# A hybrid decoder step on one core: accumulators from another PSUM pool, gate samples by pairs of heads, three output groups by ScalarE and TensorE

## The chip, the core and the metric

The kernel runs on one core of one Trainium2 chip. A core has five engines that run their own instruction queues: TensorE (PE: matrix products; its weight loads are listed apart as PEld), VectorE (DVE), ScalarE (ACT), GpSimd (POOL) and SyncE (SP, which here issues DMAs). TensorE writes its products into PSUM, eight banks of 128 partitions x 512 f32. The metric is device time in microseconds (us), from several runs; a profile is one further execution, with every instruction's start and duration.

## The reference

One layer of a decoder, D = 2048, on 256 new prompt tokens and 8 sequences of 8 new tokens each, the samples. The kernel treats the 320 tokens together.

```python
h = rms_norm(x, norm_mix_pre)
a_u, a_v, z, xbc, dt_raw = split(h @ w_in)                    # 2048 -> 9248 columns
gate_out = gelu(a_u) * (tril(W_s) @ layer_norm(gelu(a_v)) + b_s)   # 16 heads of 128, chunks of 128 tokens
ssm_out  = rms_norm_by_group(ssd_scan(silu(conv(xbc)), dt, state) * silu(z))   # 4 groups
x = x + rms_norm([gate_out | ssm_out] @ w_out, norm_mix_post)
f = (gelu(g) * u) @ w_down,   [g | u] = conv(rms_norm(x) @ w_up)    # D_FF = 5632
y = x + rms_norm(f, norm_ffn_post)
```

In the gate a sample has 8 tokens, so its mixing matrix is the upper left 8 x 8 of W_s; all samples of a head are one product with a block-diagonal 64 x 64 matrix. The outputs are y, the new states and the last rows of the convolutions and of the gate's v.

## The kernel before, in words

**Products.** Activations lie transposed (features on partitions, 320 tokens along the free dimension). Each f32 product is made of three passes on rounded parts (`accumulate`, L131): whi x xhi (L134), whi x xlo (L135), wlo x xhi (L136). Weights come in slabs of 128 x 1024 (`slab`, L109): SP loads the raw slab, ScalarE rounds it to whi (L123), VectorE takes the difference wlo (L124). A slab serves 24 passes; there are three buffers of each.

**PSUM.** Two pools of four banks each: `mm` (tag "mm", L53) and `ms` (tag "ms", L54; `misc`, L56, takes a bank of it). `mm` holds the four accumulators of a projection (`project`, L175) or, one after the other, the sixteen of an output chunk. `ms` serves the smaller products: the gate's (`sg`), those of the state scan (`xt_ps`, `s1_ps`, `yo_ps`, `cb_ps`, `up_ps`, `y_ps`), sums and spreads.

**Output chunks.** `chunk_out` (L234) multiplies four 128-row blocks of one part of the mix (or of the FFN's inner vector) with 512 rows of w_out (or w_down): for each of sixteen output blocks nb it takes an accumulator from `mm`, runs 12 passes, and VectorE adds it to `acc` (L247). Chunks 0 to 2 are the gate's first three quarters, chunk 3 its last, chunks 4 to 7 the four groups of the scan.

**Order of the work around the change.** After the gate the main line is: the convolution's input projection of group 1 (`heads_in`, through `conv_proj`, L439), chunk 3, z of group 0 (`heads_out`), projection of group 2, chunk 4, z of group 1, projection of group 3, chunk 5, z of groups 2 and 3, chunk 6, chunk 7. At the end of a `conv_proj` its four `mm` banks are taken over by `evac`: VectorE multiplies them into `pad` (L452 the prompt, L453 the samples, after which the bank is free), then ScalarE and VectorE run the convolution (L457, L459). The scan of each group (`ssd`, L888) is a background task, advanced a step at a time by `tick` between slabs; it takes `ms` banks for `ps_x`, `s1_ps` and `yo_ps` (read last by L915 and L1011) and for `up_ps` and `y_ps`. The final order on each engine is made by a planner from dependencies, priorities (`first()` is the highest) and a cost model, with the explicit `issue_after` edges.

**Gate.** `layer_norm` (L749) normalises v, tokens on partitions: `vt` has three row blocks, two of 128 prompt tokens and one of the 64 samples, of which the upper 64 partitions are zeroed once by GpSimd (L729). It goes by quarters of 512 columns (q) and row blocks (c) with two VectorE instructions each (L772, L773). `gate_mix(g, ...)` (L785) handles four heads: it loads their mixing matrices, masks them (L795 for the prompt's wT, L797 for the samples' wS, whose upper half is zero), and per head runs two prompt products (L806), one sample product of 64 columns (L807), all into one `ms` bank, and VectorE adds the bias and multiplies by u. Two heads go per step of the background task; the last group of four heads runs in one go ahead of chunk 3's projection. An f32 product that is not split into parts shows as two instructions of TensorE.

**Last norm.** In the last chunk every finished block of f is scaled by its weight and turned by VectorE into token order (`f_tok`, ten groups of 32 tokens, 128 x 512 each; `x1_tok` likewise). After the sum of squares (L1391, L1394), VectorE and ScalarE make the root r for each group (L1396 to L281). Then y = f r + x: seven groups by VectorE in one instruction each (L1417), groups 2, 5 and 8 by ScalarE (f r, L1410) and GpSimd (+ x, L1412). Each finished group is sent by a DMA (L1423), VectorE's from SP's queue and the others from ScalarE's.

Of the kernel before, what the change touches and what calls it, by code (L numbers as in the profile page):

```python
# [8 lines left out]
F32 = mybir.dt.float32  # L9
# [3 lines left out]
ALU = mybir.AluOpType  # L13
# [3 lines left out]
P = 128  # L17
NP = 256
NB, TS = 8, 8
# [14 lines left out]
def hybrid_step(  # L34
# [21 lines left out]
    def misc(name):  # L56
        return ms.tile([P, 512], F32, tag="ms", name=name)
# [173 lines left out]

        return (slice(0, P), slice(P, NT)) if nb == KD - 1 else (slice(0, NT),)

    def chunk_out(w, ck, hi, lo, begins, done=None, rate=1, apart=False):  # L234

        for nb in range(KD):
            if nb % 2 == 0:
                wb = slab(rows_of(w, 4 * ck, 4, P * nb, 256))
            ps = mm.tile([P, 512], F32, tag="mm", name=f"pd_{ck}_{nb}")
            for k in range(4):  # L240
                made = accumulate(ps[:, :NT], wb(k, nb % 2), hi[:, k, :], lo[:, k, :], k == 0, k == 3)
            with first():
                if begins:
                    act.copy(acc[:, nb, :], ps[:, :NT])
                else:
                    for ts in parts_of(nb) if apart else (slice(0, NT),):
                        added_last[:] = [dve.tensor_tensor(out=acc[:, nb, ts], in0=acc[:, nb, ts], in1=ps[:, ts], op=ALU.add).ins]  # L247
# [184 lines left out]
    with ExitStack() as mctx:  # L432
# [158 lines left out]
        with tc.tile_pool(name="gp", bufs=1) as gp:  # L591
# [157 lines left out]
            def layer_norm():  # L749

                mv = gp.tile([P, 3, 2], F32, name="mv")
                pool.memset(mv, 1.0)
                while v_task in side:
                    yield 24, 0
                for c, (o, n) in enumerate(TOK):
                    dve.bn_aggr(mv[:n, c, :], bn[c][:n].rearrange("p a b -> p (a b)"))
                lr = rsqrt_of(mv[:, :, 1], 1.0, 3)
                rows = []

                def load(q):  # L760
                    cs = slice(512 * q, 512 * q + 512)
                    for name, src in (("lg", gate_ln_g), ("lb", gate_ln_b)):
                        rows.append(gp.tile([P, 512], F32, tag=name, name=name, bufs=2))
                        with tc.issue_after(behind_r1[0]):
                            pool.dma_start(rows[-1], src[0:1, cs].broadcast_to([P, 512]))
                load(0)
                load(1)
                yield
                for q in range(4):
                    for c, (o, n) in enumerate(TOK):  # L770
                        v = vt[:n, c, 512 * q:512 * q + 512]
                        dve.scalar_tensor_tensor(out=v, in0=v, scalar=mv[:n, c, 0:1], in1=rows[2 * q][:n], op0=ALU.subtract, op1=ALU.mult)  # L772
                        dve.scalar_tensor_tensor(out=v, in0=v, scalar=lr[:n, c:c + 1], in1=rows[2 * q + 1][:n], op0=ALU.mult, op1=ALU.add)  # L773
# [10 lines left out]

            def gate_mix(g, uf, res):  # L785
                wT = gp.tile([P, 4, P], F32, tag="wT", name="wT", bufs=1)
                w8 = gp.tile([NS, 4, TS], F32, tag="w8", name="w8", bufs=1)
# [12 lines left out]
                hi, lo = out_parts(hp, "o")  # L800
                res += hi, lo
                for j in range(4):
                    fs = slice(512 * g + P * j, 512 * g + P * j + P)
                    ps = misc("sg")
                    for c in range(2):
                        pe.matmul(ps[:, P * c:P * c + P], vt[:, c, fs], wT[:, j, :], start=True, stop=True)  # L806
                    pe.matmul(ps[:, NP:NT], vt[:, 2, fs], wS[:, j].rearrange("p b t -> p (b t)"), start=True, stop=True)  # L807
                    s = tp.tile([P, NT], F32, tag="ev", name="s", bufs=2)
                    dve.tensor_tensor(out=s[:, :NP].rearrange("p (c t) -> p c t", c=2),
                                      in0=ps[:, :NP].rearrange("p (c t) -> p c t", c=2),  # L810
                                      in1=bs[:, j, :].unsqueeze(1).to_broadcast([P, 2, P]), op=ALU.add)
                    dve.tensor_tensor(out=s[:, NP:].rearrange("p (b t) -> p b t", b=NB),
                                      in0=ps[:, NP:NT].rearrange("p (b t) -> p b t", b=NB),
                                      in1=bs[:, j, :TS].unsqueeze(1).to_broadcast([P, NB, TS]), op=ALU.add)
                    dve.tensor_tensor(out=s, in0=s, in1=uf[:, j, :], op=ALU.mult)
                    split(hi[:, j, :], lo[:, j, :], s)
                    if j % 2:
                        yield

            normed = layer_norm()  # L820
            bg.append(normed)
# [32 lines left out]
        with tc.tile_pool(name="sd", bufs=1) as sd:  # L854
# [331 lines left out]
            chunk_out(w_out, 4, *res[0], False)  # L1186
            norm = heads_out(1)
            heads_in_next(3)
            finish(norm)
            chunk_out(w_out, 5, *res[1], False)  # L1190
            norm = heads_out(2)
            norm3 = heads_out(3)
            finish(norm)
            chunk_out(w_out, 6, *res[2], False)
            finish(norm3)
            finish(tasks[3])
            sq2 = hp.tile([P, NT], F32, tag="ssq", name="sq2")
# [74 lines left out]
    with tc.tile_pool(name="fp", bufs=1) as fp:  # L1272
# [129 lines left out]
        @contextmanager  # L1402
        def behind(eng):

            with tc.issue_after(taken[eng]) if eng in taken else nullcontext():
                yield

        for c in BY_POOL:
            with behind("act"):
                taken["act"] = act.activation(f[:, c], f[:, c], AF.Copy, scale=r[:, c:c + 1]).ins  # L1410
            with behind("pool"):
                taken["pool"] = pool.tensor_tensor(out=f[:, c], in0=f[:, c], in1=x[:, c], op=ALU.add).ins  # L1412
        for c in range(SN):
            if c in BY_POOL:
                continue
            with behind("dve"):
                taken["dve"] = dve.scalar_tensor_tensor(out=f[:, c], in0=f[:, c], scalar=r[:, c:c + 1], in1=x[:, c],  # L1417
                                                        op0=ALU.mult, op1=ALU.add).ins
        for eng, queue in (("sp", sp), ("act", act)):
            for c in range(SN):  # L1420
                if (c in BY_POOL) == (eng == "act"):
                    with behind(eng):
                        taken[eng] = queue.dma_start(o_y[:, c], f[:, c]).ins  # L1423


_OUTS = [
# [8 lines left out]
def laid_out(a):  # L1435
# [7 lines left out]
    def states(v, n):  # L1443
# [19 lines left out]
        "gate_w8": np.concatenate([w8] * NB),  # L1463
# [43 lines left out]
```

## Time and profile before

| | |
|---|---|
| time, median of 3 runs | 1756.57 us (1756.36 to 1757.76) |
| the profiled execution: its time / its span, first to last instruction | 1756.8 / 1755.1 us |
| granted TensorE clock, mean | 0.997 |
| HBM read / written | 280.51 / 19.69 MB |
| mean rate of the DMA queues | 172 GB/s |

The profile counts time from the first instruction. A line such as `L453 DVE TENSOR_TENSOR pad<-ps,r` is the instruction made by line 453, on VectorE, writing the tile `pad` from `ps` and `r`. "x24" is a count; what stands in square brackets is the idle time of the engine before it and the instruction whose end released it. A listed duration of a TensorE product contains its way through the array, so products overlap; the distance from one start to the next is the time that it takes from the engine.

### The profile page before, as it was taken

The numbers are of one execution on the slowest core, as the hardware profiler recorded it, in microseconds if no ns is written. First come the engines' busy times: TensorE is split into PE (matmuls) and PEld (weight loads), VectorE is DVE, ScalarE is ACT, GpSimd is POOL, SyncE is SP. The second block draws the span as 40 slices with busy tenths as digits, with TensorE's granted clock in tenths as the row PEclk, the third lists the DMA queues.
The fourth block names the chain that finished last, engine by engine and source line by source line (L and its number), as shares of the span: only waits on it lengthen the run. The fifth ranks groups of instructions, "written<-read, shape, count | busy, mean of one in ns | idle before, by whom it ended". The sixth has DMA issues, their size and how long they took to land.

```text
span 1755.1 us, 31141 instructions
## 1 busy us (share of the span) xinstructions
PE 1738.4 (99%) x12079; PEld 1720.6 (98%) x12079; DVE 1181.1 (67%) x2015; ACT 820.0 (47%) x1199; POOL 328.5 (19%) x686
## 2 busy tenths in 40 slices
PE   9999999999999999999999999999999999999996
PEld 9999999999999999999999999999999999999996
DVE  6559864656969787778855566565657565656487
ACT  6344544334656565645544434343434343343435
POOL 2532330000423323112210101010202010101003
PEclk9999999999999999999999999999999999999998
DMA  7786565456566676665654545545454545454543
GB/s 241 240 235 177 180 177 155 154 161 194 190 210 202 214 220 190 213 197 162 187 157 146 156 148 154 150 148 156 151 153 148 156 149 150 153 154 148 152 152 108
DMA packets 227171, 302.24 MB, mean 172 GB/s; under 512 B 21328, under 2 KB 151504, under 8 KB 226832
## 3 DMA queue, kind: packets, MB, share of 16 engines
q1 hardware_dynamic: 210976, 272.42, 51.1%
q0 software_dynamic: 6176, 13.84, 2.6%
q10 hardware_dynamic: 9872, 14.00, 2.2%
q8 instruction: 95, 1.56, 0.4%
q14 instruction: 52, 0.43, 0.1%
HBM read 280.51 MB, written 19.69 MB: 171 GB/s over the span
## 4 chain that ended last, share of the span: by engine, by line
PE 60%; DVE 1%; issue 0%; DVEq 0%; ACT 0%
PE ps L134 13%; PE ps L135 12%; PE ps L136 12%; PE pd L134 7%; PE pd L136 7%; PE pd L135 7%; DVE f_tok L1417 0%; PE fin_ps L1134 0%; PE y_ps L1062 0%; PE ps_one L134 0%; PE ps_other L134 0%; PE ps_one L136 0%; PE ps_other L136 0%; PE ps_other L135 0%; PE ps_one L135 0%; PE ps L188 0%
## 5 line engine op out<-in xcount | busy, mean ns | idle before, releaser
L124 DVE TENSOR_TENSOR wlo<-wraw,whi 128x1024 fp32r<-128x1024 f32 (+2 forms) x480 | 583.5, 1216 | 426.3 <-ACT whi L123 424.1
L123 ACT CAST whi<-wraw 128x1024 fp32r<-128x1024 f32 (+2 forms) x479 | 495.8, 1035 | 677.0 <-PE ps L135 390.8
L134 PE MATMUL ps<-h_hi,whi 128*128 128x320 f32 x2428 | 750.3, 309 | 0.5 <-DVE acc_mix L247 0.5
L135 PE MATMUL ps<-h_lo,whi 128*128 128x320 f32 x2428 | 748.6, 308 | 0.0
L136 PE MATMUL ps<-h_hi,wlo 128*128 128x320 f32 x2428 | 748.0, 308 | 0.0
L134 PEld LDWEIGHTS ps<-h_hi,whi 128*128 128x128 f32 x2428 | 455.7, 188 | 3.8 <-issue 0.8
L135 PEld LDWEIGHTS ps<-h_lo,whi 128*128 128x128 f32 x2428 | 455.9, 188 | 0.4
L136 PEld LDWEIGHTS ps<-h_hi,wlo 128*128 128x128 f32 x2428 | 455.7, 188 | 0.0
L136 PE MATMUL pd<-fhi,wlo 128*128 128x320 f32 x704 | 217.0, 308 | 0.0
L134 PE MATMUL pd<-fhi,whi 128*128 128x320 f32 x704 | 217.0, 308 | 0.0
L135 PE MATMUL pd<-flo,whi 128*128 128x320 f32 x704 | 217.0, 308 | 0.0
L134 PE MATMUL pd<-ohi,whi 128*128 128x320 f32 x448 | 139.0, 310 | 1.7 <-DVE pad L453 1.7
L136 PE MATMUL pd<-ohi,wlo 128*128 128x320 f32 x448 | 138.3, 309 | 0.0
L135 PE MATMUL pd<-olo,whi 128*128 128x320 f32 x448 | 138.3, 309 | 0.0
L1308 POOL COPY ptf<-pad 128x2 f32<-128x2 f32 x88 | 21.1, 240 | 600.0 <-DVE pad L1296 599.3
L134 PEld LDWEIGHTS pd<-fhi,whi 128*128 128x128 f32 x704 | 132.2, 188 | 0.0
L135 PEld LDWEIGHTS pd<-flo,whi 128*128 128x128 f32 x704 | 132.2, 188 | 0.0
L136 PEld LDWEIGHTS pd<-fhi,wlo 128*128 128x128 f32 x704 | 132.2, 188 | 0.0
L247 DVE TENSOR_TENSOR acc_ffn<-acc_ffn,pd 128x320 f32<-128x320 f32 (+1 forms) x161 | 77.1, 479 | 29.5 <-PE pd L136 28.0
L134 PEld LDWEIGHTS pd<-ohi,whi 128*128 128x128 f32 x448 | 84.1, 188 | 3.0 <-issue 1.6
L135 PEld LDWEIGHTS pd<-olo,whi 128*128 128x128 f32 x448 | 84.1, 188 | 0.3
L136 PEld LDWEIGHTS pd<-ohi,wlo 128*128 128x128 f32 x448 | 84.1, 188 | 0.0
(339 smaller groups left out, 1737.2 us busy)
## 6 DMA issues: line engine op xcount, KB each, us to landing
wraw<-in_ffn_w_up SPq DMA_DIRECT2D x176, 512.0 KB, 3.7
wraw<-in_w_in SPq DMA_DIRECT2D x132, 512.0 KB, 3.8
wraw<-in_ffn_w_down SPq DMA_DIRECT2D x88, 512.0 KB, 3.4
wraw<-in_w_out SPq DMA_DIRECT2D x64, 512.0 KB, 3.4
st<-in_state_ssm SPq DMA_DIRECT2D x40, 256.0 KB, 4.6
out_ssm_state_sample<-st ACTq DMA_DIRECT2D x30, 256.0 KB, 2.7
cs<-dacs_d SPq DMA_DIRECT2D x16, 320.0 KB, 5.1
wraw<-in_w_in SPq DMA_DIRECT2D x12, 384.0 KB, 4.4
```

Source lines behind the costliest of these rows:

```text
L123: rounded[:] = [act.copy(hi, raw).ins]
L124: dve.tensor_tensor(out=lo, in0=raw, in1=hi.bitcast(F32), op=ALU.subtract)
L134: pe.matmul(ps, whi, xhi, start=first, stop=False)
L135: pe.matmul(ps, whi, xlo, start=False, stop=False)
L136: last_made[0] = pe.matmul(ps, wlo, xhi, start=False, stop=last).ins
L247: added_last[:] = [dve.tensor_tensor(out=acc[:, nb, ts], in0=acc[:, nb, ts], in1=ps[:, ts], op=ALU.add).ins]
L1308: pool.tensor_copy(ptf[:, k, :], pad[:, 256:258])
```

## The change

Three independent edits.

1. `chunk_out` has an argument `spare`: output blocks with nb < spare take their accumulator from `ms` instead of `mm`. Chunks 3, 4, 5 and 6 are called with spare=2; the others as before.
2. In the gate the sample rows of every second head are copied to the upper 64 partitions of `vt`, beside those of the head ahead of it, by one small DMA per quarter on ScalarE's queue. The samples' mixing matrix `wS` is now block-diagonal over two heads (zeroed once as a whole), so one product of 128 columns serves both. It goes into the first head's bank; the five products of two heads are issued ahead of the element-wise work of both. The zeroing of the upper half of `vt` goes; `w8` is loaded to 128 partitions.
3. In the last norm groups 3, 6 and 9 (before: 2, 5, 8) are made without GpSimd: TensorE multiplies x by the identity into a PSUM bank, while the root is made; ScalarE scales f by r (in place); TensorE adds it to the same bank by the identity; ScalarE copies the bank back and issues the output's DMA. The order on ScalarE is written out: scale a, scale b, copy a, scale d, copy b, copy d.

```diff
-    def chunk_out(w, ck, hi, lo, begins, done=None, rate=1, apart=False):
+    def chunk_out(w, ck, hi, lo, begins, done=None, rate=1, apart=False, spare=0):
...
-            ps = mm.tile([P, 512], F32, tag="mm", name=f"pd_{ck}_{nb}")
+            ps = misc(f"pd_{ck}_{nb}") if nb < spare else mm.tile([P, 512], F32, tag="mm", name=f"pd_{ck}_{nb}")
...
-            chunk_out(w_out, 3, hi, lo, False)
+            chunk_out(w_out, 3, hi, lo, False, spare=2)
...
```

(Chunks 4, 5 and 6 likewise.)

```diff
-            wS = gp.tile([P, 4, NB, TS], F32, name="wS")
-            pool.memset(wS[NS:], 0.0)
+            wS = gp.tile([P, 2, 2, NB, TS], F32, name="wS")
+            pool.memset(wS, 0.0)
...
-            pool.memset(vt[NS:, 2], 0.0)
...
+                        if c == 2:
+                            upper_half, both_heads = (vt[rs, 2, 512 * q:512 * q + 512].rearrange("p (m i f) -> p m i f", m=2, i=2)
+                                                      for rs in (slice(NS, P), slice(0, NS)))
+                            act.dma_start(upper_half[:, :, 0], both_heads[:, :, 1])
...
-                        dve.tensor_tensor(out=wS[:NS, j], in0=w8[:, j].unsqueeze(1).to_broadcast([NS, NB, TS]),
-                                          in1=upper_s[:NS].rearrange("p (b t) -> p b t", b=NB), op=ALU.mult)
+                        rs = slice(NS * (j % 2), NS * (j % 2) + NS)
+                        dve.tensor_tensor(out=wS[rs, j // 2, j % 2], in0=w8[rs, j].unsqueeze(1).to_broadcast([NS, NB, TS]),
+                                          in1=upper_s[rs].rearrange("p (b t) -> p b t", b=NB), op=ALU.mult)
...
-                for j in range(4):
-                    fs = slice(512 * g + P * j, 512 * g + P * j + P)
-                    ps = misc("sg")
-                    for c in range(2):
-                        pe.matmul(ps[:, P * c:P * c + P], vt[:, c, fs], wT[:, j, :], start=True, stop=True)
-                    pe.matmul(ps[:, NP:NT], vt[:, 2, fs], wS[:, j].rearrange("p b t -> p (b t)"), start=True, stop=True)
+                for m in range(2):
+                    both = [misc("sg") for _ in range(2)]
+                    for i, ps in enumerate(both):
+                        j = 2 * m + i
+                        fs = slice(512 * g + P * j, 512 * g + P * j + P)
+                        for c in range(2):
+                            pe.matmul(ps[:, P * c:P * c + P], vt[:, c, fs], wT[:, j, :], start=True, stop=True)
+                        if i == 0:
+                            pe.matmul(ps[:, NP:NP + P], vt[:, 2, fs], wS[:, m].rearrange("p i b t -> p (i b t)"), start=True, stop=True)
...
```

```diff
-        BY_POOL = (2, 5, 8)
+        BY_SCALAR = (3, 6, 9)
...
-        for c in BY_POOL:
+        def scaled_by_root(c):
+
             with behind("act"):
                 taken["act"] = act.activation(f[:, c], f[:, c], AF.Copy, scale=r[:, c:c + 1]).ins
-            with behind("pool"):
-                taken["pool"] = pool.tensor_tensor(out=f[:, c], in0=f[:, c], in1=x[:, c], op=ALU.add).ins
+            with behind("pe"):
+                taken["pe"] = pe.matmul(both[c], ident, f[:, c], start=False, stop=True).ins
+
+        def taken_out(c):
+
+            with behind("act"):
+                taken["act"] = act.copy(f[:, c], both[c]).ins
+            with behind("act"):
+                taken["act"] = act.dma_start(o_y[:, c], f[:, c]).ins
+
+        both = {c: mm.tile([P, 512], F32, tag="mm", name="both") for c in BY_SCALAR}
+        taken["pe"] = made
+        for c in BY_SCALAR:
+            with behind("pe"):
+                taken["pe"] = pe.matmul(both[c], ident, x[:, c], start=True, stop=False).ins
+        a, b, d = BY_SCALAR
+        for step, c in ((scaled_by_root, a), (scaled_by_root, b), (taken_out, a), (scaled_by_root, d), (taken_out, b), (taken_out, d)):
+            step(c)
...
```

`behind(eng)` (L1403) puts an instruction behind the last one named for that engine; `made` is TensorE's last product of the sum of squares.

More of the change, by code (lines that the diff above doesn't have):

```diff
@@ L786, in gate_mix @@
                 wT = gp.tile([P, 4, P], F32, tag="wT", name="wT", bufs=1)
-                w8 = gp.tile([NS, 4, TS], F32, tag="w8", name="w8", bufs=1)
+                w8 = gp.tile([P, 4, TS], F32, tag="w8", name="w8", bufs=1)
                 bs = gp.tile([P, 4, P], F32, tag="bs", name="bs", bufs=1)
@@ L801, in gate_mix @@
                 res += hi, lo
-                for j in range(4):
-                    fs = slice(512 * g + P * j, 512 * g + P * j + P)
-                    ps = misc("sg")
-                    for c in range(2):
[L806 to L818, printed above, removed]
@@ new lines, in gate_mix @@
+                for m in range(2):
[7 more added lines that the diff above has]
+                            pe.matmul(ps[:, NP:NP + P], vt[:, 2, fs], wS[:, m].rearrange("p i b t -> p (i b t)"), start=True, stop=True)
+                    for i, ps in enumerate(both):
+                        j = 2 * m + i
+                        s = tp.tile([P, NT], F32, tag="ev", name="s", bufs=2)
+                        dve.tensor_tensor(out=s[:, :NP].rearrange("p (c t) -> p c t", c=2),
+                                          in0=ps[:, :NP].rearrange("p (c t) -> p c t", c=2),
+                                          in1=bs[:, j, :].unsqueeze(1).to_broadcast([P, 2, P]), op=ALU.add)
+                        dve.tensor_tensor(out=s[:, NP:].rearrange("p (b t) -> p b t", b=NB),
+                                          in0=both[0][:, NP + NS * i:NP + NS * i + NS].rearrange("p (b t) -> p b t", b=NB),
+                                          in1=bs[:, j, :TS].unsqueeze(1).to_broadcast([P, NB, TS]), op=ALU.add)
+                        dve.tensor_tensor(out=s, in0=s, in1=uf[:, j, :], op=ALU.mult)
+                        split(hi[:, j, :], lo[:, j, :], s)
+                    yield
@@ L1185, in hybrid_step @@
             finish(norm)
-            chunk_out(w_out, 4, *res[0], False)
+            chunk_out(w_out, 4, *res[0], False, spare=2)
             norm = heads_out(1)
@@ L1189, in hybrid_step @@
             finish(norm)
-            chunk_out(w_out, 5, *res[1], False)
+            chunk_out(w_out, 5, *res[1], False, spare=2)
             norm = heads_out(2)
@@ L1193, in hybrid_step @@
             finish(norm)
-            chunk_out(w_out, 6, *res[2], False)
+            chunk_out(w_out, 6, *res[2], False, spare=2)
             finish(norm3)
@@ L1406, in behind @@
                 yield
[L1408 removed]
+        def scaled_by_root(c):
             with behind("act"):
                 taken["act"] = act.activation(f[:, c], f[:, c], AF.Copy, scale=r[:, c:c + 1]).ins
[L1411 to L1412 removed]
+            with behind("pe"):
[13 more added lines that the diff above has]
+            step(c)
         for c in range(SN):
[L1414 removed]
+            if c in BY_SCALAR:
                 continue
@@ L1418, in hybrid_step @@
                                                         op0=ALU.mult, op1=ALU.add).ins
[L1419 to L1423, printed above, removed]
+        for c in range(SN):
+            if c not in BY_SCALAR:
+                with behind("sp"):
+                    taken["sp"] = sp.dma_start(o_y[:, c], f[:, c]).ins
 _OUTS = [
@@ L1462, in laid_out @@
         "gate_wT": w_s.transpose(2, 0, 1),
-        "gate_w8": np.concatenate([w8] * NB),
+        "gate_w8": np.concatenate([w8] * 2 * NB),
         "gate_b_s": a["gate_b_s"], "ssm_dt_bias": a["ssm_dt_bias"], "ssm_a_log": a["ssm_a_log"],
```

## The prediction

> **What bounds the kernel now.** I read the page first, then TensorE's own waits, then the busy time by stretch. PE is TensorE, PEld its weight loads, DVE VectorE, ACT ScalarE, POOL GpSimd.
>
> ```profile
> span 1755.1 us, 31141 instructions
> PE 1738.4 (99%) x12079; PEld 1720.6 (98%) x12079; DVE 1181.1 (67%) x2015; ACT 820.0 (47%) x1199; POOL 328.5 (19%) x686
> ```
> ```profile
> PE pd L134 <- DVE pad L453: 1.7, 2, 1.4
> PE ps L134 <- DVE acc_mix L247: 0.5, 1, 0.5
> ```
> ```profile
> 860.00:1739.80 879.80, 879.80 (x6001) 879.80 (x6000) 549.09 (x917) 368.66 (x472) 120.15 (x349) 1.00 0.49 149
> 1739.80:1755.10 15.30, 1.98 (x9) 0.98 (x7) 11.19 (x19) 3.18 (x7) 5.08 (x3) 0.71 0.46 171
> ```
>
> TensorE is the bound: from 860.00 to 1739.80 it has no idle time (the columns are length, then PE, PEld, DVE, ACT, POOL busy, granted clock, DMA share, GB/s). Only three things can move the end: fewer TensorE instructions, TensorE's rare waits (the second list: line, us in total, times, longest), and the last 15.30 us, in which TensorE is busy 1.98 us. The change touches one of each, so it is worth a few us of 1755 at most. About 0.2% (3.5 us) is what a measurement of this kernel can tell from no change.
>
> **1. Output chunks that begin on two other banks.** Chunks 3 to 6 take their first two accumulators (pd) from the pool ms instead of mm. The stall is at chunk 4; TensorE there, then VectorE:
>
> ```profile
> 548.25 0.31 PE L136 MATMUL ps<-h_hi,wlo 128*128 128x320 f32 x1
> 549.97 0.39 PE L134 MATMUL pd<-ohi,whi 128*128 128x320 f32 x1 [1.41 <-DVE pad L453]
> 550.34 0.31 PE L136 MATMUL pd<-ohi,wlo 128*128 128x320 f32 x1
> ...
> 555.20 0.31 PE L136 MATMUL pd<-ohi,wlo 128*128 128x320 f32 x1
> 555.76 0.39 PE L134 MATMUL pd<-ohi,whi 128*128 128x320 f32 x1 [0.25 <-DVE pad L453]
> ...
> 557.60 0.63 PE L998 MATMUL up_ps<-xsp,bm 128*128 128x512 f32 x2
> ```
> ```profile
> 547.27 2.08 DVE L124 TENSOR_TENSOR wlo<-wraw,whi 128x1024 fp32r<-128x1024 f32 x1
> 549.61 0.21 DVE L453 TENSOR_TENSOR pad<-ps,r 128x64 f32<-128x64 f32 x1
> ...
> 551.39 0.21 DVE L453 TENSOR_TENSOR pad<-ps,r 128x64 f32<-128x64 f32 x1
> ...
> 555.41 0.21 DVE L453 TENSOR_TENSOR pad<-ps,r 128x64 f32<-128x64 f32 x1
> 555.54 1.21 DVE L124 TENSOR_TENSOR wlo<-wraw,whi 128x1024 fp32r<-128x1024 f32 x1
> 556.67 0.47 DVE L247 TENSOR_TENSOR acc_mix<-acc_mix,pd 128x320 f32<-128x320 f32 x1
> ```
>
> A product follows the one before it by 0.147 us (879.80 / 6001). The first of chunk 4 comes 1.72 us after the last of the convolution, so 1.57 us are lost; 555.20 to 555.76 loses 0.41 more, and the product after a stop runs 0.08 longer (0.39 against 0.31). The releases are the four evacuations (L453) of the convolution's banks, the fourth ending at 555.62.
>
> With spare banks the chunk may begin at 548.40. What is late next is the weights: the third product (L136) needs wlo, which VectorE ends at 547.27 + 2.08 = 549.35. It starts about 549.4 instead of 550.34, so 0.9 of the 1.57 us goes and the rest becomes a wait for wlo. From there 12 products a block (1.76 us): the third block starts at about 552.6 on the bank freed at 549.82, the fourth at 554.4 (freed 551.60). The up_ps pair (0.47) follows; then the fifth at 556.6 (its wlo ends 556.75, its third product comes at 556.9) and the sixth at 558.4, both on banks free by 555.62. No block waits, so the 0.41 and its 0.08 go as well: 1.4 us for chunk 4. Chunk 3 has a smaller stop:
>
> ```profile
> 457.01 0.31 PE L136 MATMUL pd<-ohi,wlo 128*128 128x320 f32 x1
> 457.39 0.39 PE L134 MATMUL pd<-ohi,whi 128*128 128x320 f32 x1
> ```
>
> That is 0.38 - 0.15 + 0.08 = 0.3 us, gone by the same reasoning. Chunks 5 and 6 have no row among TensorE's waits, so nothing is won there. **Sum: 1.7 us.** Bounds: 2.4 if VectorE's order also brings that wlo forward (all of 1.57 + 0.41 + 0.08 + 0.3); 0 if VectorE, not the banks, sets the pace. What it costs: the two ms banks are held until VectorE's sums (L247; chunk 4's first at 556.67), while the pair up_ps at 557.60 wants two of the four. Two are left, so it does not wait.
>
> **2. Gate samples two heads at a time.** Of 16 small products of 64 columns, eight of 128 columns remain. An f32 product is two instructions.
>
> ```profile
> 249.46 0.33 PE L807 MATMUL sg<-wS,vt 128*128 128x64 f32 x2
> 249.63 0.66 PE L806 MATMUL sg<-wT,vt 128*128 128x128 f32 x4
> 250.13 0.33 PE L807 MATMUL sg<-wS,vt 128*128 128x64 f32 x2
> ```
> ```profile
> sum 10.09, PE 10.09; mean PE 1.44
> ```
> ```profile
> 421.66 1.03 PE L412 MATMUL xt_ps<-ident,xs 128*128 128x128 f32 x8
> 422.53 0.61 PE L950 MATMUL cb_ps<-cT,bT 128*128 128x128 f32 x4
> ```
>
> Starts tell the price: a 64-column pair takes 0.17 us (249.46 to 249.63), a 128-column instruction 0.87 / 8 = 0.109. The gate's seven stretches on TensorE, six of two heads (the first runs from 249.02 to 250.27) and the last of four, sum to 10.09 us. After, each step of two heads has ten instructions of 128 columns, 80 in all: 8.7 us. **Sum: 1.4 us less**, all on the path, since TensorE is the bound there. Bounds: 0.1 at the 0.125 us that an L806 takes behind a 64-column pair (0.50 / 4, 10.0 us for 80), and 1.8 if width is free (rival c). I take the row in which 128 columns follow 128. The Trainium skill, "TensorE: Matmul & The Clock Gate", section LDWEIGHTS, gives a load of 128 weight columns as 128/1.2 = 107 ns, however little is streamed through them; by it 16 loads fewer save an estimated 1.7 us. The trace does not bear that out: 64-column instructions follow one another by 85 ns (0.17 / 2).
>
> Added: four DMAs on ScalarE's queue that copy the second head's sample rows to the upper half, each behind the row group's last L773.
>
> ```profile
> L773 DVE SCALAR_TENSOR_TENSOR vt<-vt,rs_r,lb x12: 734/739/749, 157.1 to 185.4; 128x512 f32<-128x512 f32 x8, 64x512 f32<-64x512 f32 x4
> DMA to landing us min/median/max: 4.7/4.7/4.7
> ```
>
> The last can start at about 186 and, at the 4.7 us of the neighbouring store (L777), lands near 191; the first gate product is at 249. That cover is 58 us; without it a DMA would cost its 4.7 us once. Queued behind each on ScalarE are weight casts (L123); the wait is at most one L773 (0.74 us), and TensorE's list has no wait in that stretch: nothing. A memset of POOL (L729) goes, off the path: nothing. VectorE's masks and sums keep their count.
>
> **3. The tail.** Two halves: who computes, and how fast the output leaves.
>
> ```profile
> L1417 DVE SCALAR_TENSOR_TENSOR f_tok<-f_tok,rs_r,x_tok x7: 739/752/1755, 1743.8 to 1750.8; 128x512 f32<-128x512 f32 x7
> ```
> ```profile
> L1412 POOL TENSOR_TENSOR f_tok<-f_tok,x_tok x3: 1707/1711/1742, 1744.6 to 1747.9; 128x512 f32<-128x512 f32 x3
> ```
> ```profile
> 1745.40:1751.20 5.80, 0.00 (x0) 0.00 (x0) 5.80 (x5) 0.31 (x1) 4.24 (x3) 0.57 0.84 314
> 1751.20:1753.41 2.21, 0.00 (x0) 0.00 (x0) 0.32 (x1) 0.00 (x0) 0.00 (x0) 0.50 0.97 361
> ```
>
> VectorE takes 0.74 us for a group, but 1.75 for those beside GpSimd's three. Without GpSimd its seven run 1743.77 to about 1749 instead of 1751.5. The win is not 2.5 us, because the output becomes the bound: the ten groups of 128 x 512 f32 are 2.62 MB, and at the 361 GB/s of the stretch with a full queue they take 7.26 us; from the same first byte at 1745.40 it ends at 1752.66 instead of 1753.41. **Sum: 0.75 us**, with the closing 1.69 us (1755.10 - 1753.41) unchanged.
>
> ScalarE's three groups must be ready before that backlog ends:
>
> ```profile
> L1410 ACT ACTIVATE f_tok<-f_tok,rs_r x3: 707/707/722, 1743.8 to 1745.0; 128x512 f32<-128x512 f32 x3
> ```
> ```profile
> 807.58 1.88 PE L1134 MATMUL fin_ps<-x1s,btok 128*128 128x512 f32 x4
> ```
>
> An f32 product of 512 columns is 0.94 us (1.88 / 2). The three x products run 1741.85 to 1744.7, beside the root. Then scale, product, copy (a copy taken as long as a scale, 0.71): the first copy ends near 1746.4, the second near 1747.8, the third near 1749.2, so the last data can flow near 1750, 0.85 us behind their issue as the first output's do (1743.77 + 0.75 to 1745.40), and are not the end. Two us more would still be hidden behind the backlog. Bounds: 2.5 (VectorE's own gain) and -2.1. The latter is this: the rows above give a granted clock (third column from the end) of 0.57 and 0.50 while TensorE idles; were all six products at half, 1.88 us each, the last copy would end at 1741.85 + 6 x 1.88 + 0.71 = 1753.9 and its data, 0.85 + 0.73 later, at 1755.5. I take full clock, since TensorE comes to these products straight from 880 us without a pause.
>
> **Total:** 1.7 + 1.4 + 0.75 = 3.85 us. Span 1755.10 to 1751.25. The profiled execution took 1756.8, 1.7 over its span, and stands 0.23 above the median 1756.57; off the median that gives **1752.7 us**.
>
> **Rivals.** (a) *Banks were not the limit in chunk 4*: VectorE is busy nearly throughout there, and TensorE, earlier by the gate's gain, meets wlo late again. Against: the list names pad, not wlo. For: that wlo ends only 1.0 us before its use (549.35, 550.34). Then part 1 gives about 0.2: 1754.2. (b) *The tail gives nothing*, since the scale-product-copy chain has five hand-overs and its third group could end last, 2.6 us later than I have it: 1753.5. (c) *Width is free in the gate*: if a weight load sets a small product's pace, the kept one stays at 0.17 us though twice as wide, and the removed one's 0.17 goes whole, with the 0.06 by which the L806 behind it is slower (0.50 against 4 x 0.109): 8 x 0.23 = 1.8 us, 1752.3. Against: 85 ns for 64 columns, 109 for 128. (The Trainium skill's LDWEIGHTS rule is of this kind.) (d) *The change does not do what it says*: the order on every engine is planned anew, and a wait like that of L247 (0.5) may appear twice or vanish: 1752.2 to 1753.7. (e) *Slower*: ms is no free pool. Its four banks hold the state products (ps_x twice, s1_ps, yo_ps) until VectorE's L1011:
>
> ```profile
> 445.60 0.86 DVE L1011 TENSOR_TENSOR xdt<-yo_ps,ed 64x256 f32<-64x256 f32 x2
> ```
> ```profile
> 451.87 0.31 PE L134 MATMUL pd<-ohi,whi 128*128 128x320 f32 x1
> ```
>
> They are free at 446.5, 5.4 us before chunk 3 wants one. If the new plan puts L1011 behind the chunk's evacuations, the second block, due 1.76 us after 451.87, waits from 453.6 until those end (457.24, where TensorE restarts at 457.39) and the two L1011 have run (0.86): 4.7 us. 1756.57 - 3.85 + 4.7 = 1757.4, and 1766.8 if chunks 4 and 5 do the same. It decides from L1011 later than 453.6.
>
> **How the numbers follow.** Forecast 0.54, (a) 0.14, (b) 0.08, (c) 0.09, (d) 0.09, (e) 0.06. Faster means under 1753.06, only 0.36 above the forecast, whose own spread I take as 0.8 either side, from the bounds of the three terms: 0.39 of its 0.54 lies below, with (c) and two thirds of (d) 0.54. Slower is (e) where it repeats, 0.05. The rest, 0.41, lies within 0.2%, (a) and (b) among it. The range is 1751.2 (1.8 for the gate, 2.4 for the banks, 0.75 for the tail, 0.4 of (d)) to 1755.2 (gate 1.4 alone): (e) and the far ends stay outside.
>
> **What would show it.** Part 1: no wait of pd on pad L453, a short gap ahead of chunk 4's third product, up_ps near 1.4 us earlier behind the convolution. Part 2: steps of two heads of 1.1 us. Part 3: seven equal DVE steps of 0.74, DMA full from 1745.4 on, closing 1.69 unchanged. Wrong if TensorE waits on ms or wlo elsewhere, or if ScalarE's third group is the last to leave.

## The result, and the profile after

The changed kernel takes 1751.39 us (median of 7 runs, 1750.76 to 1753.16) against 1756.61 beside it (7 runs, 1755.48 to 1757.76): the ratio is 0.9971, with a 95% interval of 0.9961 to 0.9981, so 5.2 us less. The forecast was 1752.7, 3.9 us less. Its direction and range hold, and in the profiled execution each of its three terms came out larger than forecast.

The page of the changed kernel, span and busy times (TensorE's instructions fall by 4: sixteen samples' instructions go, twelve of the last norm come), and then what TensorE waits for (line, us in total, times, longest; a wait of 1.1 us at the start, the same in both kernels, is left out):

```profile
span 1749.7 us, 31126 instructions
PE 1741.7 (100%) x12075; PEld 1721.0 (98%) x12075; DVE 1181.5 (68%) x2015; ACT 821.5 (47%) x1202; POOL 317.8 (18%) x682
```
```profile
PE both L1421 <- ACT f_tok L1419: 1.0, 1, 1.0
PE ps L134 <- DVE acc_mix L247: 0.3, 1, 0.3
PE tsum L289 <- DVE sq L1276: 0.2, 1, 0.2
```

The wait of pd on pad (1.7 us) is gone, as the forecast asked, and nothing on wlo or on an ms bank took its place. Where the time went is read by pairing TensorE's long products in both traces, in order, and taking start before minus start after. That difference moves in a few places only:

| where | us won | forecast |
|---|---|---|
| first 10 us (differs from run to run) | 0.17 | - |
| gate | 1.83 | 1.4 |
| chunk 3 | 0.33 | 0.3 |
| chunk 4 | 2.16 | 1.4 |
| elsewhere up to the last product (0.10 at 517 us, the rest behind chunk 4) | -0.39 | 0 |
| behind the last product | 1.3 | 0.75 |
| sum, against 1755.1 - 1749.7 | 5.4 | 3.85 |

The start of that last product, in the kernel before and in the changed one, carries the first five lines (4.10 us):

```profile
1739.88 0.31 PE L136 MATMUL pd<-fhi,wlo 128*128 128x320 f32 x1
```
```profile
1735.78 0.31 PE L136 MATMUL pd<-fhi,wlo 128*128 128x320 f32 x1
```

**Gate.** TensorE in the changed kernel at the step shown before (start, duration, ... , count):

```profile
248.83 0.61 PE L812 MATMUL sg<-wT,vt 128*128 128x128 f32 x4
249.27 0.39 PE L814 MATMUL sg<-wS,vt 128*128 128x128 f32 x2
249.49 0.61 PE L812 MATMUL sg<-wT,vt 128*128 128x128 f32 x4
249.86 0.39 PE L134 MATMUL ps<-h_hi,whi 128*128 128x320 f32 x1
```

From 248.83 to 249.86 are 1.03 us, against 1.25 before (249.02 to 250.27): 0.22 less for two heads, 0.23 by the paired starts, where 0.17 (1.4 / 8) had been forecast. The reason stands in a row that the forecast had not read, the weight loads (PEld) of the same steps. Before, and then after:

```profile
248.88 0.56 PEld L806 LDWEIGHTS sg<-wT,vt 128*128 128x128 f32 x4
249.35 0.30 PEld L807 LDWEIGHTS sg<-wS,vt 128*128 128x128 f32 x2
249.57 0.53 PEld L806 LDWEIGHTS sg<-wT,vt 128*128 128x128 f32 x4
250.02 0.30 PEld L807 LDWEIGHTS sg<-wS,vt 128*128 128x128 f32 x2
250.24 0.19 PEld L134 LDWEIGHTS ps<-h_hi,whi 128*128 128x128 f32 x1
```
```profile
249.16 0.30 PEld L814 LDWEIGHTS sg<-wS,vt 128*128 128x128 f32 x2
249.38 0.53 PEld L812 LDWEIGHTS sg<-wT,vt 128*128 128x128 f32 x4
249.83 0.19 PEld L134 LDWEIGHTS ps<-h_hi,whi 128*128 128x128 f32 x1
```

Two loads take 0.22 us (249.35 to 249.57, 250.02 to 250.24) and four take 0.45 (249.57 to 250.02): 0.111 us for each load. After the change it is the same 0.22 for the pair that now streams 128 columns (249.16 to 249.38). So the pace is the load's, and 128 columns cost what 64 did. The token sums (L289), which stream one column, have loads 0.112 us apart in the trace of the kernel before. It is no fixed price of any instruction: loads of 64 columns in the same trace come in twos, 0.055 us apart (L953, at 423.07 and 423.13 us). Nor is any width free: an instruction of 512 columns took 0.47 us in the row of L1134 that the forecast shows.

**Chunk 4.** TensorE across the seam between convolution and chunk 4, then VectorE and GpSimd, in the changed kernel:

```profile
546.02 0.31 PE L136 MATMUL ps<-h_hi,wlo 128*128 128x320 f32 x1
546.17 0.31 PE L134 MATMUL pd<-ohi,whi 128*128 128x320 f32 x1
```
```profile
542.23 1.94 DVE L400 SCALAR_TENSOR_TENSOR olo<-xs,prm,ohi 128x320 fp32r<-128x320 f32 x4
544.08 1.22 DVE L124 TENSOR_TENSOR wlo<-wraw,whi 128x1024 fp32r<-128x1024 f32 x1
```
```profile
544.59 2.65 POOL L1000 TENSOR_TENSOR st<-st,tote 128x512 f32<-128x512 f32 x2 [14.88 <-DMA st<-in_state_ssm]
```

The chunk follows by 0.15 us, without a gap, and the wlo that the forecast had late is ready at 545.30, before the chunk begins. In the kernel before, the same two VectorE rows were longer, 2.73 us and 2.08 (the latter is in the prediction), and GpSimd's pair lay across both:

```profile
544.62 2.73 DVE L400 SCALAR_TENSOR_TENSOR olo<-xs,prm,ohi 128x320 fp32r<-128x320 f32 x4
```
```profile
545.85 2.43 POOL L992 TENSOR_TENSOR st<-st,tote 128x512 f32<-128x512 f32 x2 [13.91 <-DMA st<-in_state_ssm]
```

VectorE lost 0.79 + 0.86 = 1.65 us there, about as much as TensorE then waited. What releases GpSimd's pair is the DMA that brings the state (the square brackets of its rows). The experiments below take this up.

**Tail.** VectorE's groups in the changed kernel, ScalarE's third copy, and busy time by stretch (length; PE, PEld, DVE, ACT, POOL busy; granted clock, DMA share, GB/s):

```profile
L1442 DVE SCALAR_TENSOR_TENSOR f_tok<-f_tok,rs_r,x_tok x7: 746/746/752, 1739.7 to 1743.6; 128x512 f32<-128x512 f32 x7
```
```profile
1744.54 0.58 ACT L1426 COPY f_tok<-both 128x512 f32<-128x512 f32 x1 [0.74 <-PE both L1421]
```
```profile
1741.29:1748.34 7.05, 2.25 (x5) 0.49 (x3) 3.10 (x5) 2.36 (x4) 0.00 (x0) 0.88 1.00 372
```
```profile
1748.34:1749.70 1.36, 0.00 (x0) 0.00 (x0) 0.00 (x0) 0.00 (x0) 0.00 (x0) 0.50 0.00 0
```

The seven steps are equal and 0.75 us each; the output runs at full share from its first byte to its last (7.05 us instead of 8.01), and 1.31 us close the kernel instead of 1.69 (the last stretch above reaches 0.05 us past the end of the span, 1749.65). ScalarE's third group is ready at 1745.12, when a backlog of 3.2 us of output lies ahead of the end.

### The profile page after: what moved, and what is told of

The parts are those of the page before. It is cut to its first block, busy times and chain, and to the rows that moved or that the text cites. A ratio compares the mean times of both kernels' runs of the same rounds, so it can differ in the third digit from the quotient of the medians.

```text
span 1749.7 us, 31126 instructions
## 1 busy us (share of the span) xinstructions
PE 1741.7 (100%) x12075; PEld 1721.0 (98%) x12075; DVE 1181.5 (68%) x2015; ACT 821.5 (47%) x1202; POOL 317.8 (18%) x682
## 4 chain that ended last, share of the span: by engine, by line
PE 59%; DVE 1%; ACT 0%; DMA 0%; issue 0%; ACTq 0%; DVEq 0%; SPq 0%
PE ps L134 12%; PE ps L135 12%; PE ps L136 12%; PE pd L134 7%; PE pd L136 7%; PE pd L135 7%; DMA wraw<-in_ffn_w_up 0%; DVE wlo L124 0%; PE fin_ps L1142 0%; PE y_ps L1070 0%; PE ps_other L135 0%; PE ps_other L136 0%; PE ps_other L134 0%; PE both L1421 0%; ACT whi L123 0%
## 5 line engine op out<-in xcount | busy, mean ns | idle before, releaser
L124 DVE TENSOR_TENSOR wlo<-wraw,whi 128x1024 fp32r<-128x1024 f32 (+2 forms) x480 | 583.6, 1216 | 421.2 <-ACT whi L123 418.5
```

Of the source, the lines that this page charges most:

```text
L124: dve.tensor_tensor(out=lo, in0=raw, in1=hi.bitcast(F32), op=ALU.subtract)
```

## The experiments

Theory: the three edits pay independently; chunk 4's share comes from the banks, the gate's from fewer instructions, the tail's from an output without gaps. The rivals were that VectorE, not the banks, sets chunk 4's pace, and that the new order of all engines, not the edits, does it.

### The three edits one by one

The first edit alone (`spare=2` for chunks 3 to 6, all else as before):

```diff
+            ps = misc(f"pd_{ck}_{nb}") if nb < spare else mm.tile([P, 512], F32, tag="mm", name=f"pd_{ck}_{nb}")
```

> The kernel before with edit 1 alone (spare=2 for chunks 3 to 6). Theory A (the edits meet in chunk 4): without the gate's 1.8 us VectorE reaches chunk 4's first wlo only after GpSimd's pair L992, so the wait for pad becomes a wait of about 0.6 us for wlo ahead of the third product; chunk 4 gains 1.3 to 1.5 us, chunk 3 0.3, in all about 1.7 us, 1754.9. Rival B (the banks were worth 2.5 us by themselves): no wait at chunk 4, 2.5 us, 1754.1. Rival C (the new order on VectorE did it): wlo ends before 547 here too although GpSimd's pair stands where it stood.

Measured: 1754.79 us (11 runs), ratio 0.9993 (0.9984 to 1.0003); span 1752.8. By TensorE's starts, chunk 3 gives 0.33 and chunk 4 gives 2.16, with no wait on wlo: the step of 0.67 us that the forecast had kept as a wait for wlo isn't there. VectorE's L400 and L124 take 1.94 and 1.22 us in this run too. All five engines run the same instructions in the same order as before, so a new order isn't the cause.

The gate's edit alone (two heads in a product of 128 columns):

> The kernel before with edit 2 alone (samples of two heads in one product). Theory: each step of two heads takes 1.02 to 1.03 us of TensorE instead of 1.25 and the last 2.14 instead of 2.59, 1.8 us in all, and with VectorE ahead of GpSimd at chunk 4 its banks come free earlier too, so up to 1 us more there: 1753.8 to 1754.8. Rival (the gain of 1.4 that was forecast, the rest owed to the other edits): 1755.2.

Measured: 1754.85 us (11 runs), ratio 0.9991 (0.9983 to 1.0000); span 1753.1. The gate gives its 1.83 us, and then chunk 3 takes back 1.93 of it, with two waits of TensorE where the kernel before had one of 0.3:

```profile
450.69 0.39 PE L134 MATMUL pd<-ohi,whi 128*128 128x320 f32 x1 [0.78 <-DVE pad L453]
...
457.19 0.39 PE L134 MATMUL pd<-ohi,whi 128*128 128x320 f32 x1 [0.98 <-DVE pad L453]
```

At chunk 4, on the other hand, 1.58 us are won in this run, though all chunks use the four old banks, and VectorE's L124 takes 1.22 us there. So the banks can't be all of it. By the sum this run looks like a gate that pays in full (2.03 us at the last product); place by place, chunk 3 spends the gate's gain, and chunk 4 brings in another.

The tail alone (groups 3, 6, 9 by ScalarE and TensorE):

> The kernel before with edit 3 alone. Theory: the stretch behind the last product of the last chunk shrinks from 15.2 to 13.9 us: 1.0 by the output that leaves in 7.05 us at 372 GB/s instead of 8.0, 0.3 by a shorter closing; 1755.3. Rival (a part of that came from the rest of the change): 0.75 us, 1755.9.

Measured: 1755.8 us (11 runs), ratio 0.9995 (0.9986 to 1.0004); span 1754.1. The work behind the last product takes 14.14 us instead of 15.21: the output 7.06, the closing 1.57. The stall at chunk 4 stays, and VectorE's slow rows with it (2.74 and 2.08 us).

### The tail without ScalarE and TensorE

The changed kernel with all ten groups by VectorE:

```diff
-        BY_SCALAR = (3, 6, 9)
+        BY_SCALAR = ()
```

> The changed kernel, but VectorE makes all ten groups of the last norm; no ScalarE, TensorE or GpSimd, all outputs from SP's queue. Theory (the output's DMAs are the bound once GpSimd is out): ten groups at 0.66 us keep up with ten transfers at 0.705, so the last byte leaves within 0.2 us of the changed kernel's, 1751.4. Rival (sharing the groups is what pays): the last group comes 3 x 0.66 = 2 us later, 1752.5 to 1753.4.

Measured: 1751.73 us (7 runs), ratio 0.9974 (0.9964 to 0.9985). Its VectorE rows and its output:

```profile
L1420 DVE SCALAR_TENSOR_TENSOR f_tok<-f_tok,rs_r,x_tok 128x512 f32<-128x512 f32 x10 | 6.7, 747 | 0.0
```
```profile
1740.65:1747.65 7.00, 0.00 (x0) 0.00 (x0) 5.08 (x8) 0.00 (x0) 0.00 (x0) 0.50 1.01 374
```

VectorE is 2 us longer at it and the output ends as it did (7.00 us, closing 1.31). So what pays in the tail is that GpSimd leaves. The path through ScalarE and TensorE is not needed: VectorE's ten steps overlap and take 6.7 us together, 0.67 us a group, and the output needs 0.70 us a group.

### What a narrow gate product costs

The changed kernel with the paired product cut back to 64 columns:

```diff
-pe.matmul(ps[:, NP:NP + P], vt[:, 2, fs], wS[:, m].rearrange("p i b t -> p (i b t)"), start=True, stop=True)
+pe.matmul(ps[:, NP:NP + NS], vt[:, 2, fs], wS[:, m, 0].rearrange("p b t -> p (b t)"), start=True, stop=True)
```

> The changed kernel, with the instruction that makes the samples of two heads cut back to the first head's 64 columns: it leaves out the second head's samples, which are taken from the first's. Theory (each instruction of this form costs TensorE one weight load, whose starts stand 0.111 us apart, whatever its width): the steps of two heads stay as long as in the changed kernel, 1.03 us from the first instruction of one to the first of the next, and TensorE's work behind the gate starts when it did, within 0.1 us. Rival (the forecast's pace: 128 columns cost 0.109 us and 64 columns 0.085): each step gets 0.05 us shorter, 0.4 us over the eight; second rival (time goes with the columns, 0.43 ns for one): 0.055 us shorter for each step.

TensorE at the same step, its products and then its weight loads:

```profile
248.89 0.61 PE L812 MATMUL sg<-wT,vt 128*128 128x128 f32 x4
249.34 0.33 PE L814 MATMUL sg<-wS,vt 128*128 128x64 f32 x2
249.51 0.66 PE L812 MATMUL sg<-wT,vt 128*128 128x128 f32 x4
249.93 0.39 PE L134 MATMUL ps<-h_hi,whi 128*128 128x320 f32 x1
```

```profile
249.23 0.30 PEld L814 LDWEIGHTS sg<-wS,vt 128*128 128x128 f32 x2
249.45 0.53 PEld L812 LDWEIGHTS sg<-wT,vt 128*128 128x128 f32 x4
249.90 0.19 PEld L134 LDWEIGHTS ps<-h_hi,whi 128*128 128x128 f32 x1
```

Measured: 1751.31 us (one run), span 1749.6; by the starts the gate gives 1.83 us, as in the changed kernel. The step takes 1.04 us (248.89 to 249.93) against 1.03 with 128 columns. The 64-column pair looks cheap by its own starts (249.34 to 249.51, 0.17 us), but what it seems to save is paid by the instruction behind it. Its two loads take 0.22 us as before. The load sets the pace; both rivals fall.

### Who makes VectorE late: GpSimd's state products

The kernel before, with its four banks, less the pair of products by which GpSimd scales one state at 545.85:

```diff
-                    if n in shrinks:
+                    if n in shrinks and (g, n) != (1, 8):
```

> The kernel before, without the two products by which GpSimd scales one state at 545.85 us (it leaves that state unscaled). Theory (VectorE's steps at 544.6 to 549.3 us took 1.65 us longer than the same steps elsewhere because GpSimd's pair ran beside them, and what TensorE waited for at the third product of chunk 4 stood behind them): the four steps of L400 take 1.94 us instead of 2.73, the step of L124 behind them 1.22 instead of 2.08, and the wait of 1.4 us at chunk 4 is gone or below 0.2 us, with the four banks as they were; 0.5 us or more of the time is won. Rival (four banks are too few there, as the forecast had it, and VectorE's delay adds little to it): the wait stays at 1 us or more.

VectorE in the same steps:

```profile
542.35 1.94 DVE L400 SCALAR_TENSOR_TENSOR olo<-xs,prm,ohi 128x320 fp32r<-128x320 f32 x4
544.20 1.22 DVE L124 TENSOR_TENSOR wlo<-wraw,whi 128x1024 fp32r<-128x1024 f32 x1
```

Among TensorE's waits none on pad is left. Its starts gain 2.16 us at chunk 4, what the changed kernel gains there, with the banks as they were; span 1752.0, time 1753.7 (one run; 0.97 us of its gain lie in the first 10 us, which differ from run to run). The stall was four banks and VectorE's 1.65 us together: either one removed is enough to lift it or most of it.

This run also wins 0.33 us at chunk 3, with four banks and with nothing changed before 545 us: against TensorE, VectorE was 0.8 us earlier there (its fourth L453 starts at 455.43 instead of 457.03, TensorE 0.79 earlier). The tail alone, with four banks too, loses 0.12 us more at chunk 3 than the kernel before. So what stands at chunk 3 in the table cannot be put down to the spare banks.

Then the gate's edit alone, less the six products by which GpSimd scales three states at 438.4 to 446.7:

```diff
-                    if n in shrinks:
+                    if n in shrinks and (g, n) not in ((0, 0), (0, 2), (0, 5)):
```

> The gate's edit alone, as in the second run, without the six products by which GpSimd scales three states of the first group at 438.4 to 446.7 us (it leaves those three states unscaled). Theory (what VectorE loses beside GpSimd's products is what made it late at chunk 3, as it was at chunk 4): its step of L124 beside them takes 1.22 us instead of 1.94, its steps up to 448.7 us end 2 us sooner or more, both waits of chunk 3 (1.1 and 1.3 us from the end of one product to the start of the next) are gone or below 0.3 us together with four banks, and the last product starts 1.5 us sooner or more than in that run. Rival (VectorE simply has too much to do there, whoever runs beside it): its steps are no shorter by more than 0.7 us in all, and at least 1 us of the two waits stays.

VectorE with the six products beside it, and without:

```profile
438.56 1.94 DVE L124 TENSOR_TENSOR wlo<-wraw,whi 128x1024 fp32r<-128x1024 f32 x1 [0.37 <-ACT whi L123]
440.54 2.92 DVE L942 TENSOR_TENSOR xsp<-xq,xsp 64x512 fp32r<-64x512 f32 x2
```
```profile
438.76 1.23 DVE L124 TENSOR_TENSOR wlo<-wraw,whi 128x1024 fp32r<-128x1024 f32 x1
440.02 1.29 DVE L942 TENSOR_TENSOR xsp<-xq,xsp 64x512 fp32r<-64x512 f32 x2
```

Both waits of chunk 3 are gone (0.99 + 1.22 us by the starts; the wait of 0.3 on pad that is left is at chunk 4's fifth block, 552.42), span 1751.6 instead of 1753.1, time 1753.31 (one run). So chunk 3 in the second run had the same cause. In the changed kernel VectorE is as slow there (1.97 us for that L124) and TensorE does not wait: there it is the spare banks that hide it.

### One bank, and a first group in halves

The changed kernel with `spare=1`:

> The changed kernel, with one product of each chunk on the other banks instead of two. Theory (VectorE is 1 us late at chunk 3, and one bank more covers 2.6 us, that is one product): no wait for a pad at chunk 3 or 4, the last product starts within 0.3 us of the changed kernel's. Rival (the wait at chunk 3 is at the fourth product or later, which one bank moves by one product but does not remove): a wait of some 0.5 to 1 us comes back at chunk 3.

Measured: span 1750.4, time 1752.11 (one run). TensorE lists no wait on a pad; by the starts chunk 3 loses 0.2 us and chunk 4 nothing. The last product is 0.73 us later than in the changed kernel, outside the 0.3 expected, by a wait on ev (L390) in z of group 1 at 517 us. The order on all engines is the same. VectorE was 0.9 us later there from 510 us on: its L124 waits for ScalarE, and ScalarE for a DMA (cs from dacs_d, L1049 at 507.91 instead of 506.97). Why that DMA came later stays open.

The changed kernel with its first output group scaled and sent in two halves:

```diff
-                taken["dve"] = dve.scalar_tensor_tensor(out=f[:, c], in0=f[:, c], scalar=r[:, c:c + 1], in1=x[:, c],
-                                                        op0=ALU.mult, op1=ALU.add).ins
...
+            return [slice(0, W // 2), slice(W // 2, W)] if c == 0 else [slice(0, W)]
```

> The changed kernel, with the first of the ten output groups scaled, added and sent in two halves of 256 columns. Theory (from its first byte on the output runs at full rate, so only the first byte's time and the bytes count): the first byte leaves about 0.35 us sooner (half of a 0.75 us VectorE step), the last byte as much sooner, and the whole gets 0.3 us shorter, 1751.1 us. Rival (something else than the bytes sets the end: ScalarE's third group is ready last): the last byte leaves when it did, 12.55 us behind the last product, and a gap shows in the output. Second rival: transfers of 1 KB in each row run below the rate of those of 2 KB, which gives back about 0.1 us of it.

Measured: 1751.94 us (7 runs), ratio 0.9972 (0.9960 to 0.9983): nothing won. The first byte leaves 0.26 us sooner behind the last product (5.25 instead of 5.51 us) and the last one 0.1 later. The first stretch of the output, from 0.09 us ahead of its first byte, shows where it goes:

```profile
1741.50:1742.60 1.10, 1.10 (x4) 0.38 (x2) 1.10 (x3) 0.50 (x2) 0.00 (x0) 1.00 0.72 238
```

The two halves, 1 KB to a partition, leave at 238 GB/s over this stretch, against 372. Finer stretches of the trace divide that. While the queues are full, the halves move at 338 GB/s (share 1.00, from 1741.65 to 1741.95 and from 1742.15 to 1742.45). In between the queues run dry twice (share 0.52 from 1741.95 to 1742.15, 0.39 from 1742.45 to 1742.70), since a half is out before the next piece, issued 0.41 and 0.65 us later, reaches them. So the output takes 7.41 us instead of 7.05, which eats the 0.26 us. The theory's "from its first byte on the output runs at full rate" failed. The second rival's 0.1 us is about right for the slower rate (262 KB at 338 instead of 372 GB/s are 0.07 us more); the larger part is the dry queues, which neither had.

This run shows something else. GpSimd's pair came across VectorE's L400 again:

```profile
542.25 2.74 DVE L400 SCALAR_TENSOR_TENSOR olo<-xs,prm,ohi 128x320 fp32r<-128x320 f32 x4
544.91 2.08 DVE L124 TENSOR_TENSOR wlo<-wraw,whi 128x1024 fp32r<-128x1024 f32 x1
```
```profile
546.21 0.31 PE L135 MATMUL pd<-olo,whi 128*128 128x320 f32 x1
547.05 0.41 PE L136 MATMUL pd<-ohi,wlo 128*128 128x320 f32 x1 [0.53 <-DVE wlo L124]
547.30 0.31 PE L134 MATMUL pd<-ohi,whi 128*128 128x320 f32 x1
```

Here, with the banks spare, is the wait for wlo that the forecast had described: the two steps take 0.84 and 0.25 us instead of 0.147 each, so 0.80 are lost. The banks alone are then worth 2.16 - 0.80 = 1.36 us at chunk 4 (forecast: 1.4), and the other 0.80 us depend on who comes first. Over ten traces: where GpSimd's pair starts 1.15 to 1.23 us after the first L400 (the kernel before, the tail alone, and this one) VectorE takes 2.08 us for that L124; where it starts 1.44 to 2.36 us after (the seven others) VectorE takes 1.22. Between the two lies the start of the fourth L400, 1.38 us after the first: a pair that comes ahead of it holds it up (1.35 us instead of 0.55), one that comes behind does not. In all ten the pair starts 0.12 to 0.16 us after the DMA with its state has landed, 3.1 us after that DMA's issue in this run and 4.0 in the kernel before and the changed one. So the order at chunk 4 is a race between that DMA and VectorE.

## Why the prediction was right, and where its terms were off

**What bounds the kernel** held: TensorE sets the end, and the three places were the ones that moved. Each edit alone gives less than 0.1%, which the intervals of its runs don't tell from nothing; by the spans of the profiled executions they are 2.3, 2.0 and 1.0 us, against 5.4 together.

**Term 1, the banks (1.7 forecast, 2.5 measured).** The mechanism held, and for the order of events that the forecast took from the kernel before, so did the size at chunk 4: where the pair comes ahead again, in the run with halves, the banks give 1.36 us and the wait for wlo is there. The other 0.80 us are luck of the profiled execution, in which the state's DMA came behind and wlo was ready in time. None of the three edits decides that order: the run with halves has all three and the pair ahead, the first edit alone has the pair behind. What the forecast missed is that there was a race: it carried over the wlo that ended at 549.35, quoted the row of 2.08 us for that L124, while the same form stood at 1.21 us in its own fence, and did not ask what lay beside it. It was GpSimd's pair. Chunk 3's 0.3 has the right size, but a run with four banks has it too, so that the banks give it is not shown. Rival (a), that VectorE sets the pace, named half of the cause and expected a smaller gain (0.2); VectorE was late only beside GpSimd. Of rival (d), the first edit alone shows the same gain at chunk 4 with the order unchanged. The gate's edit does change the order, on VectorE from its 80th instruction on, and what that alone costs or gives is not shown. Rival (e) did not come: no run lists a wait on an ms bank that the state products hold.

The Trainium skill, "SBUF — State Buffer", section "SBUF: two separate sides", says that GpSimd and a VectorE instruction with two SBUF inputs share a port pair which whoever starts first holds for its whole instruction. The traces agree: beside GpSimd's 1.2 us products VectorE's L124 takes 2.08 us instead of 1.22, beside its 1.7 us sums an output group takes 1.75 instead of 0.75, and where VectorE comes first GpSimd's pair takes up to 3.57 us instead of 2.43.

**Term 2, the gate (1.4 forecast, 1.83 measured).** The step that failed is "Starts tell the price: a 64-column pair takes 0.17 us". The start of the product behind a narrow one comes early and the one after it late; the price is read from the starts of the weight loads, 0.111 us each. Sixteen loads fewer are 1.78 us. Rival (c) was the right one, with the right size (1.8). The forecast also said of the Trainium skill's rule for a weight load ("TensorE: Matmul & The Clock Gate", section LDWEIGHTS, 107 ns for 128 weight columns, with no term for what is streamed) that the trace did not bear it out. It does: the measured pace is 111 ns, and the run with 64 columns has the same step. "All on the path" did not hold for the edit alone: there chunk 3 takes all of it back.

**Term 3, the tail (0.75 forecast, 1.3 measured).** That the output becomes the bound was right, and so were ScalarE's copies: the forecast had the third end near 1749.2, 9.3 us behind the last product, and it ended 1745.12, as far behind its own. Two sizes were off. The rate is 372 GB/s and not 361, since the stretch it was taken from had a share of 0.97 and not of 1.00 (7.05 us instead of 7.26). The closing was taken as unchanged and fell from 1.69 to 1.31 us. It is 1.69 or 1.70 in all five traces with GpSimd's sums and 1.26 to 1.57 in the others; why was not tried. The forecast's "two us more would still be hidden" is not tested by a later ScalarE; in the all-VectorE tail VectorE's part takes 2 us longer, and the output ends as it did. The half clock of the lower bound did not come: the granted clock was 1.00 from 1735 to 1744.6 us, and the last of the products ends at 1744.50.

**What stays open.** The 0.39 us that TensorE loses elsewhere (0.47 at the token sums at 850 us, where the other runs lose up to 0.22, and 0.19 won at 684); why the DMA with the state lands when it does, and how often each order comes, since each kernel has one trace; and why single runs of the changed kernel reach 1753.16, since those runs left no trace.

## What to carry to other kernels

Before a stall is put down to buffers, compare the duration of the late engine's rows with the same form elsewhere: a row at 1.7 times its usual time can point to a neighbour, here GpSimd, and taking that neighbour's products away was worth as much as the buffers. Read the price of small TensorE products, here up to 128 columns, from the starts of their weight loads, and count loads, not columns. A gain on the bounding engine ahead of a tight seam must be followed to that seam, since it may be spent there as a wait.

## What the runs showed of the hardware

A weight load of 128 columns for an f32 instruction came every 0.111 us, and the instruction streamed 64 or 128 columns at that price. Output at full queues left at 372 to 374 GB/s in pieces of 2 KB to a partition, and at 338 in pieces of 1 KB. Two GpSimd products of 1.2 us cost VectorE 1.65 us, and nothing where they started 0.2 us later (1.44 us behind the first L400, not 1.23). TensorE kept a granted clock of 1.00 for the products behind its last long stretch, and the clock was at 0.50 in the closing stretch.
